# Layer 1's convolved inputs by seven block products instead of eight, and the norm ahead of the split

## The chip, the core and the metric

One core of a Trainium2 chip runs the whole program, two decoder layers for 528 positions. The metric is the device time of one execution in microseconds, the median of three runs. Five engines take part: PE (TensorE, matmuls), DVE (VectorE) and ACT (ScalarE) for element-wise work, POOL (GpSimd) and SP (SyncE), which issues nearly all DMAs. Each engine takes its instructions in the order in which they were placed on its queue, and waits at an instruction until what it needs is there.

## What is computed

16 meta positions are put ahead of 512 real ones (T = 528), the model width is 2048, all in float32. Layer 0 mixes with an S5 and an mLSTM branch; the change leaves it as it was up to its last output projection. Layer 1 is a Mamba-2 mixer:

```python
def ssd_layer(x, norm_g, w_in, conv_w, conv_b, dt_bias, a_log, d, gnorm, w_out):
    p = (rmsnorm(x, norm_g) @ w_in).astype(F32)
    z, xbc, dt = jnp.split(p, [SSD_INNER, SSD_INNER + SSD_CONV_DIM], axis=-1)
    xbc = jax.nn.silu(causal_dwconv(xbc, conv_w.astype(F32), conv_b.astype(F32)))
    xs, bm, cm = jnp.split(xbc, [SSD_INNER, SSD_INNER + SSD_GROUPS * SSD_STATE], axis=-1)
    ...
    def step(state, inp):
        xc, dtc, bc, cc = inp
        cum = jnp.cumsum(dtc * a, axis=1)
        seg = jnp.exp(jnp.where(causal, cum[:, :, None] - cum[:, None], -jnp.inf))
        cb = jnp.einsum('btgn,bsgn->btsg', cc, bc)
        w = cb[..., None] * seg * dtc[:, None]
        y = (jnp.einsum('btsgr,bsgrp->btgrp', w, xc)
             + jnp.exp(cum)[..., None] * jnp.einsum('btgn,bgrpn->btgrp', cc, state))
        ...
    y = y * silu(z); y = groupwise rmsnorm(y) * gnorm
    return x + y @ w_out
```

(The last two lines are shortened.) SSD_INNER is 4096; there are 8 groups, each with one tile of b, one of c, four of x and four of z, a tile being 128 channels by 528 positions. The states advance over chunks of 16, 128, 128, 128 and 128 positions. A final rmsnorm follows, and the meta positions are dropped.

## The kernel before

Channels lie on partitions, positions in the free dimension. A matmul operand of float32 is held as a high part `h` (rounded to fp32r) and a remainder `l`, and a product is three matmuls: h by h, h by l, l by h. So an activation `x` is a tile of 128 x 2 x 528, and a weight tile of 128 x 1024 (eight contraction tiles) is loaded as `wraw`, cast by ACT to `wh` and subtracted by DVE to `wl` (`wload`, L114), each with three buffers. `gemm` (L135) makes one output tile of 128 channels: 16 contraction tiles x two halves of 264 positions x three matmuls = 96 matmuls into two PSUM banks `g` of the pool `psg`, which has three; the banks are then emptied by the caller's `evac`.

The instructions' order on every queue is fixed when the program is built, by a planner that lists the program with a model of each engine's time; `tc.high_priority(offset=...)` pulls a piece forward in that list. What the code writes one after the other is therefore interleaved: in layer 1 PE's queue runs one group's SSD matmuls among the projection matmuls of z and of the next group.

*The seam.* `last0` (L1040) receives each of 16 output tiles of layer 0: it stores the stream, multiplies by the norm's weight `gp1` and splits the result at once into `x`, and adds the squares to `acc1`. The reciprocal root mean square `rstd` is known only after the last tile: a matmul with `ones` sums `acc1` over partitions (L1052), ACT takes the root and DVE the reciprocal. Since `x` is left unnormed, all projections run without waiting for `rstd`, and each evacuation multiplies by it: `xf<-g,rstd` (L1124), `zr<-g,rstd` (L1223). The first projection is dt's, 64 rows wide (L1091), then b, c and the four x tiles of group 0.

*A group.* `ssd_group_in` (L1129) calls `xbc` (L1121) for b, c and four x tiles: 96 matmuls, evacuation into `xf`, then the causal convolution and SiLU. c has only 516 positions, two halves of 258. `ssd_group` (L1147) transposes b and x on PE, builds the states, and then for each of four channel tiles i: a DMA brings the running sums of two heads, broadcast to all partitions, into `cr` (128 x 1024, two buffers, L1193 and 1195); DVE subtracts (`wexp<-cumc,cr`, L1199), ACT applies Relu and Exp, DVE multiplies by `cbm`; PE forms `p<-wexp,xdt` (L1206) and `p<-bc,state` (L1210); ACT makes `ecum`, the exponential of cr (L1212, 1213); DVE puts the two halves together into `yss` (L1215 to 1217). `ssd_out` (L1226) multiplies by the gate z, whose projection `ssd_z` (L1221) PE runs in between, and norms the group. Groups 0 to 6 run so in turn; group 7 runs beside the output projection.

Of the kernel before, what the change touches and what calls it, by code (L numbers as in the profile page):

```python
# [11 lines left out]
F32 = mybir.dt.float32  # L12
# [8 lines left out]
T = SEQ + N_META  # L21
# [3 lines left out]
REAL = ((N_META, SEQ),)  # L25
RMS_EPS, HEAD_EPS = 1e-6, 1e-5
# [15 lines left out]
def hybrid_trunk(ctx: ExitStack, tc: tile.TileContext, io, out):  # L42
# [931 lines left out]
    def out_steps(op, w, ys, k0, nk, cols, src, dst, between=lambda m: None, beside=1, ws={}, upto=KD):  # L974
# [3 lines left out]
        while todo:  # L978
            ms = [todo.pop(0) for _ in range(beside)]
            rs = []  # L980
            for _ in ms:
                res = op.tile([128, T], F32, tag="res", bufs=2, name="res")
                move(res[:, :n], src(_))
                rs.append(res)
# [13 lines left out]
            yield  # L998

# [16 lines left out]
    def fillers():  # L1016
# [5 lines left out]
        yield from out_steps(op, io["wo0"], ya, 0, 8, FULL, lambda m: io["hT"][:, m], lambda m, r_: move(o1D[:, m], r_), lambda m: len(yb) < 8 and load_b(m))  # L1022
# [3 lines left out]
        yield from out_steps(op, io["wo0"], yb, 8, 6, FULL, lambda m: o1D[:, m], lambda m, r_: move(o2D[:, m], r_), lambda m: [load_c(m) for _ in range(2) if len(yc) < 12], ws=ws)  # L1026
# [13 lines left out]
    def last0(m, res):  # L1040
        move(hD[:, m], res)
        x = xp.tile([128, 2, T], F32R, tag="x", name="x")
        split(x, res, gp1[:, m:m + 1])
# [5 lines left out]
    out_part(op, io["wo0"], yc, 20, 6, FULL, lambda m: o2D[:, m], last0)  # L1049
    ss = pair()  # L1050
    for hf, (c0, cn) in enumerate(FULL):
        mm(ss[:, hf, :cn], ones, acc1[:, c0:c0 + cn], True, True)  # L1052
    rstd_of(halves(rstd), ss[:, :, :HALF], 1.0 / D_MODEL, halves(acc1))
    p2.close()
    op_.close()
    xs = xs1

# [5 lines left out]
    op1 = o1.enter_context(tc.tile_pool(name="out1", bufs=1, reuse_waits="tile"))  # L1063
    p3 = ExitStack()
# [26 lines left out]
    gemm([io["wdt"]], xs, lambda hf, c0, cn, p: mul(xd[:, c0:c0 + cn], p, rstd[:SSD_H, c0:c0 + cn]), m=64, nk=16)  # L1091
# [25 lines left out]


    C_COLS = ((12, 258), (270, 258))

    def xbc(m, tag, bufs, cols=FULL):  # L1121
        xf = qp.tile([128, T + 3], F32, tag="xf", bufs=2, name="xf")
        G.memset(xf[:, 0:3 + cols[0][0]], 0.0)  # L1123
        gemm(w1(32 + m), xs, lambda hf, c0, cn, p: mul(xf[:, 3 + c0:3 + c0 + cn], p, rstd[:, c0:c0 + cn]), cols=cols)  # L1124
        o = qp.tile([128, T], F32, tag=tag, bufs=bufs, name=tag)
        conv_silu(xf, cw1[:, m], cb1[:, m:m + 1], o, True)
        return o

    def ssd_group_in(g):  # L1129
        b = xbc(32 + g, "bc", 4)  # L1130
# [305 lines left out]
```

## Time and profile before

| | us |
|---|---|
| median of three runs | 2892.97 (2890.85 to 2894.90) |
| the profiled execution | 2893.52 |
| its span | 2891.8 |
| PE busy in the span | 2853.4 (99%) |
| DVE busy | 2033.8 (70%) |
| ACT busy | 1240.7 (43%) |
| the seam: last matmul of layer 0 starts | 1451.47 |
| b and c of group 0 done | 1487.22 |
| one of five like groups of layer 1 | 131.5 |

The profile is that of one execution; times inside it are counted from its span's start. Records of one engine may overlap by some 0.1 us where they follow each other, and a matmul's record is longer than the distance to the next one, because matmuls are pipelined; the cost of a matmul is the distance. An F32 matmul leaves two records. The matmul clock that was granted stands beside each stretch as a share of 2.4 GHz.

### The profile page before, as it was taken

The page shows a single profiled execution, that of the slowest core. Times are in us where ns is not written, and L with a number is a line of the kernel's source. Part 1 is how long each engine was busy: PE and PEld are TensorE (multiplying, and loading weights), DVE is VectorE, ACT ScalarE, POOL GpSimd, SP SyncE. Part 2 cuts the span into 40 slices and gives each one's busy share as a digit, 9 for nine tenths or more (in the row PEclk, how much of TensorE's full clock was granted, in tenths as well). Part 3 has the DMA queues.
Part 4 walks back from the last instruction along what each step waited for, and adds up shares of the span by engine and source line. Part 5 has one row for each costly group of instructions (what it writes and reads, how often), then busy time and mean ns, then how long its engine had stood idle before and what let it go on. Part 6 is the DMA issues. An engine that isn't in the chain of part 4 may idle for free.

```text
span 2891.8 us, 50753 instructions
## 1 busy us (share of the span) xinstructions
PE 2853.4 (99%) x20483; PEld 2638.5 (91%) x20483; DVE 2033.8 (70%) x3343; ACT 1240.7 (43%) x2118; POOL 268.1 (9%) x550
## 2 busy tenths in 40 slices
PE   8999999999999999999999999999999999999998
PEld 8999999999999999999998989898998989788887
DVE  8998889889867766754466776767676767663333
ACT  7554445444336645533333443434352534332222
POOL 3122211220001111100000000000000000000000
PEclk9999999999999999999999999999999999999999
DMA  5333333333345666565543323333232323355433
GB/s 194 113 113 114 112 125 112 107 108 117 118 168 168 208 206 207 166 191 168 157 102 105 124 95 110 102 103 112 88 122 81 126 90 121 123 166 179 153 119 114
DMA packets 155599, 383.73 MB, mean 133 GB/s; under 512 B 18964, under 2 KB 37396, under 8 KB 155364
## 3 DMA queue, kind: packets, MB, share of 16 engines
q1 hardware_dynamic: 153188, 378.39, 40.9%
q8 instruction: 161, 2.64, 0.4%
q10 hardware_dynamic: 2176, 2.10, 0.2%
q14 instruction: 74, 0.61, 0.1%
HBM read 320.22 MB, written 60.20 MB: 132 GB/s over the span
## 4 chain that ended last, share of the span: by engine, by line
PE 86%; DMA 4%; DVE 4%; ACT 2%; issue 2%; POOL 1%; SPq 0%; DVEq 0%; ACTq 0%; POOLq 0%
PE g L74 76%; PE p L74 5%; PE s L74 2%; DMA wraw<-in_wo 1%; PE p L1206 1%; PE s L430 1%; DVE nm L47 1%; PE p L1171 1%; DVE nm L65 1%; ACT w L68 1%; DVE wl L47 1%; ACT wh L119 0%; DMA wraw<-in_w 0%; PE p L556 0%; DMA ae<-rowD 0%
## 5 line engine op out<-in xcount | busy, mean ns | idle before, releaser
L74 PE MATMUL g<-x,wh 128*128 128x264 f32 (+2 forms) x10176 | 2111.2, 303 | 14.7 <-ACT wh L286 5.8
L74 PEld LDWEIGHTS g<-x,wh 128*128 128x128 f32 x10176 | 1629.0, 188 | 96.5 <-issue 17.6
L74 PE MATMUL g<-x,wl 128*128 128x264 f32 (+2 forms) x5088 | 1534.4, 302 | 0.2 <-DVE wl L47 0.2
L74 PEld LDWEIGHTS g<-x,wl 128*128 128x128 f32 x5088 | 956.5, 188 | 33.8 <-issue 2.3
L119 ACT CAST wh<-wraw 128x1024 fp32r<-128x1024 f32 (+1 forms) x435 | 441.9, 1017 | 919.6 <-PE g L74 680.6
L47 DVE TENSOR_TENSOR wl<-wraw,wh 128x1024 fp32r<-128x1024 f32 (+2 forms) x444 | 529.9, 1194 | 266.0 <-ACT wh L119 261.9
L74 PE MATMUL g<-y,wh 128*128 128x264 f32 (+2 forms) x1312 | 296.3, 321 | 0.0
L74 PEld LDWEIGHTS g<-y,wh 128*128 128x128 f32 x1312 | 217.8, 188 | 20.2
L74 PE MATMUL g<-y,wl 128*128 128x264 f32 (+2 forms) x656 | 211.9, 323 | 0.0
L65 DVE SCALAR_TENSOR_TENSOR acc<-xf,cw,acc 128x528 f32<-128x528 f32 x216 | 172.8, 800 | 4.9 <-ACT acc L68 1.2
L47 DVE TENSOR_TENSOR res<-g,res 128x264 f32<-128x264 f32 (+2 forms) x129 | 62.8, 489 | 117.6 <-PE g L74 112.6
L74 PEld LDWEIGHTS g<-y,wl 128*128 128x128 f32 x656 | 123.4, 188 | 9.1
L47 DVE TENSOR_TENSOR xf<-g,rstd 128x264 f32<-128x264 f32 (+1 forms) x142 | 59.6, 424 | 84.8 <-PE g L74 84.4
L68 ACT ACTIVATE wexp<-wexp 128x1024 f32<-128x1024 f32 x64 | 67.7, 1058 | 53.3 <-DVE wexp L47 51.4
L418 ACT CAST us<-hl 32x264 fp32r<-32x264 f32 x192 | 78.8, 411 | 6.3 <-PE p L74 3.5
L1123 POOL MEMSET xf<- 128x3 f32 (+1 forms) x48 | 5.0, 105 | 714.9 <-DVE acc L65 508.7
L68 ACT ACTIVATE acc<-xf,cb,cw 128x528 f32<-128x528 f32 x72 | 59.4, 825 | 26.8 <-DVE xf L47 26.8
L47 POOL TENSOR_TENSOR dec<-decx,dec 128x512 fp32r<-128x512 f32 (+1 forms) x32 | 46.9, 1464 | 240.9 <-ACT dec L1178 240.9
L47 DVE TENSOR_TENSOR y<-wraw,y 128x512 fp32r<-128x512 f32 (+1 forms) x28 | 19.5, 699 | 65.6 <-ACT y L126 65.5
L68 ACT ACTIVATE tab<-tab,ec 128x32 f32<-128x32 f32 (+3 forms) x128 | 41.5, 331 | 48.8 <-POOL tab L47 48.8
L68 ACT ACTIVATE x<-acc 128x528 f32<-128x528 f32 x32 | 20.6, 645 | 80.2 <-DVE acc L65 80.2
L47 DVE TENSOR_TENSOR acc<-g,rstd 128x264 f32<-128x264 f32 (+1 forms) x64 | 28.0, 437 | 35.9 <-PE g L74 35.3
(1000 smaller groups left out, 3092.1 us busy)
## 6 DMA issues: line engine op xcount, KB each, us to landing
wraw<-in_w SPq DMA_DIRECT2D x285, 512.0 KB, 3.5
wraw<-in_wo SPq DMA_DIRECT2D x80, 512.0 KB, 4.0
wraw<-in_wo SPq DMA_DIRECT2D x64, 384.0 KB, 3.6
cr<-cumD SPq DMA_DIRECT2D x32, 512.0 KB, 4.7
zD<-s SPq DMA_DIRECT2D x32, 264.0 KB, 2.0
y1D<-yss SPq DMA_DIRECT2D x32, 256.0 KB, 2.1
wraw<-y1D SPq DMA_DIRECT2D x32, 256.0 KB, 2.9
xcD<-xc SPq DMA_DIRECT2D x24, 264.0 KB, 2.1
```

Of the source, the lines that this page charges most:

```text
L47: (eng or V).tensor_tensor(out=out, in0=a, in1=b, op=op)
L65: V.scalar_tensor_tensor(out=out, in0=a, scalar=s, in1=b, op0=op0, op1=op1)
L68: S.activation(out=out, in_=a, func=func, **kw)
L74: PE.matmul(o, lhsT=w, rhs=x, start=start, stop=stop)
L119: S.copy(h[:, :n], raw[:, :n])
L418: S.copy(us[32 * n:32 * n + 32, q], hl[rows, a].bitcast(F32))
L430: PE.matmul(yps[32 * q:32 * q + 32, :HALF], lhsT=c[:, n, 32 * q:32 * q + 32], rhs=x[:, n], start=n == 0, stop=n == 1, tile_position=(0, 32 ...
L1123: G.memset(xf[:, 0:3 + cols[0][0]], 0.0)
L1171: PE.transpose(out=o[:, 128 * i:128 * i + 128], in_=x[i][:, s0:s0 + sn_], identity=ident)
L1206: PE.matmul(yp[64 * r_:64 * r_ + 64, 0, 128 * ch:128 * ch + 128], lhsT=xdt[:, ch, 64 * (2 * i + r_):64 * (2 * i + r_) + 64], rhs=w[:, r_, ...
```

## The change

Three things are changed, all in layer 1 and at its beginning.

1. The norm is applied to the stream. `last0` keeps `x` as plain F32 (no split). After the last tile, `rstd` is made in two halves, dt's projection runs with F32 operands from the unnormed x (32 matmuls into a `p` pair, in the place of 96 into `g`), and then each of the 16 tiles is multiplied by `rstd` (`normed`) and split (`finish`). The evacuations multiply by nothing; z's `silu2` reads PSUM directly.
2. b and c, and the x tiles two by two, are made in pairs by `gemm_pair`. Two output tiles by two halves of positions by two blocks of contraction tiles (three tiles each, NP = 3) is a 2 x 2 by 2 x 2 block product; it is formed by seven block products in Winograd's arrangement. It needs four combinations of x (made once, tiles `t`, by twelve differences `tr` and their splits) and four of the weights (`wsum`, five DVE operations of 384 columns a pair, then splits of 768). The other 10 contraction tiles are added in as before. The banks are asked for one at a time: p1, p2, p3, p6, p7, p5, p4, q4. 23 pairs are made so; b and c of group 0 are made in the old way, without pairs.
3. Buffers shrink to make room: `cr` has one buffer and its exponential is written into it (`ecum` is gone), `bc` has three for four, `yss` four for five, `decx` shares with `ysqa`, `res` of the last projection shares with `t`.

Cut to its core:

```diff
     def last0(m, res):
         move(hD[:, m], res)
-        x = xp.tile([128, 2, T], F32R, tag="x", name="x")
-        split(x, res, gp1[:, m:m + 1])
+        x = xp.tile([128, T], F32, tag="x", name="x")
+        act(x, res, AF.Identity, scale=gp1[:, m:m + 1])
...
-    rstd_of(halves(rstd), ss[:, :, :HALF], 1.0 / D_MODEL, halves(acc1))
+    with tc.high_priority(offset=1500):
+        for hf, (c0, cn) in enumerate(FULL):
+            c_ = slice(c0, c0 + cn)
+            mm(ss[:, hf, :cn], ones, acc1[:, c_], True, True)
+            rstd_of(rstd[:, c_], ss[:, hf, :cn], 1.0 / D_MODEL, acc1[:, c_])
...
+    dps = pair()
+    for k, x in enumerate(xs1):
+        for hf, (c0, cn) in enumerate(FULL):
+            mm(dps[:SSD_H, hf, :cn], wdt[:, k], x[:, c0:c0 + cn], k == 0, k == KD - 1)
...
+        for k in range(NP):
+            a, b = normed(k, "xf", 2), normed(k + NP, "bc", 3)
+            finish(k, a)
+            finish(k + NP, b)
+            tr = qp.tile([128, 4, HALF], F32, tag=("xdt", "state")[k % 2], name="tr")
+            sub(tr[:, 0], a[:, HALF:], a[:, :HALF])
...
+            split(t, tr)
+            tf.append(t)
+        for k in range(2 * NP, KD):
+            finish(k, normed(k, *(("xf", 2), ("bc", 3))[k % 2]))
...
+        p1 = bank()
+        prod(p1, g1, 0, xq(0, lo), True, True)
+        with tc.high_priority(offset=1500):
+            S.copy(f2[:, hi], p1[:, :HALF])
+        p2, p3 = bank(), bank()
...
+        g3 = wpart(s2s4, 2 * NS)
+        p6 = bank()
+        prod(p6, g3, 0, tq(1), True, True)
+        evac(f2[:, hi], f2[:, hi], p6)
+        prod(p3, g3, NS, xq(1, hi), False, True)
+        evac(f1[:, hi], f2[:, hi], p3)
...
+        p7, p5 = bank(), bank()
+        prod(p7, g4, 0, tq(2), True, True)
+        evac(f2[:, lo], f2[:, hi], p7)
+        prod(p5, g4, NS, tq(0), True, True)
+        evac(f1[:, hi], f1[:, hi], p5)
...
     def ssd_group_in(g):
-        b = xbc(32 + g, "bc", 4)
-        c = xbc(40 + g, "bc", 4, C_COLS)
+        b, c = xbc((32 + g, 40 + g), "bc", 3, g == 0)
+        x = xbc((4 * g, 4 * g + 1), "x2", 6) + xbc((4 * g + 2, 4 * g + 3), "x2", 6)
...
-            cr = qp.tile([128, 2, 4, 128], F32, tag="cr", bufs=2, name="cr")
+            cr = qp.tile([128, 2, 4, 128], F32, tag="cr", bufs=1, name="cr")
...
-            ec_ = qp.tile([128, SEQ], F32, tag="ecum", bufs=1, name="ecum")
-            act(ec_[0:64], cr[0:64, 0].rearrange("p c t -> p (c t)"), AF.Exp)
+            ec_ = cr[:, 0].rearrange("p c t -> p (c t)")
+            act(ec_[0:64], ec_[0:64], AF.Exp)
...
-        gemm(w1(m), xs, lambda hf, c0, cn, p: mul(z, p, rstd[:, c0:c0 + cn]), cols=REAL)
-        silu2(z, z, th)
+        gemm(w1(m), xs, lambda hf, c0, cn, p: silu2(z, p, th), cols=REAL)
```

How the instructions stand on the queues shows at two places. On PE at the seam, before, the sum of squares (`p<-acc,ones_r`) stands deep among dt's narrow matmuls (`g<-x,wh 64x264`):

```order
L74 MATMUL g<-x,wh 64x264 x2
L74 MATMUL g<-x,wl 64x264
L74 MATMUL g<-x,wh 64x264
L74 MATMUL p<-acc_16474,ones_r 128x264 x2
L74 MATMUL g<-x,wh 64x264
```

After, on the same engine and place, from the last matmuls of layer 0 (`g<-y_16471`) to the first of b:

```order
L76 MATMUL g<-y_16471,wh 128x264 x2
L76 MATMUL g<-y_16471,wl 128x264
L76 MATMUL p<-acc_16474,ones_r 128x264
L76 MATMUL p<-x,wdt 64x264 x11
L76 MATMUL p<-acc_16474,ones_r 128x264
L76 MATMUL p<-x,wdt 64x264 x21
L76 MATMUL g<-x,wh 128x264 x4
```

The first sum of squares now stands directly behind layer 0's last matmul, with nothing between it and the addition into acc that it reads.

On DVE in the middle of a steady group's core, before (`yss<-p,ecum` begins the use of one product of the four, `wexp<-cumc,cr` the making of a decay matrix from a loaded cr):

```order
L47 TENSOR_TENSOR yss<-p,ecum 128x512
L47 TENSOR_TENSOR zr<-g,rstd 128x512
L47 TENSOR_TENSOR yss<-yss,p 128x512
L47 TENSOR_TENSOR wexp<-cumc,cr 128x1024
L65 SCALAR_TENSOR_TENSOR yss<-x_22418,dsk,yss 128x512
L65 SCALAR_TENSOR_TENSOR zr<-zth,zr 128x512
L47 TENSOR_TENSOR yss<-p,ecum 128x512
L47 TENSOR_TENSOR wl<-wraw,wh 128x1024
L47 TENSOR_TENSOR yss<-yss,zr 128x512
L47 TENSOR_TENSOR wexp<-cumc,cr 128x1024
```

After, between the second and the third product of a group (`xf<-xf,g` is an addition that empties a bank of a pair, `wl<-wsum,wh` the split of a weight sum):

```order
L49 TENSOR_TENSOR yss<-p,cr 128x512
L49 TENSOR_TENSOR yss<-yss,p 128x512
L49 TENSOR_TENSOR xf<-xf,g 128x264
L67 SCALAR_TENSOR_TENSOR yss<-x_22567,dsk,yss 128x512
L49 TENSOR_TENSOR yss<-yss,zr 128x512
L49 TENSOR_TENSOR wexp<-cumc,cr 128x1024
L49 TENSOR_TENSOR wl<-wsum,wh 128x768
L49 TENSOR_TENSOR ysqa<-ysqa,zth 128x512
L49 TENSOR_TENSOR wl<-wraw,wh 128x640
L49 TENSOR_TENSOR wexp<-wexp,cbm 128x1024
```

Before, a decay matrix is begun while products that use the other cr buffer are still to come; after, each `wexp<-cumc,cr` stands behind the `yss<-p,cr` that frees the one buffer, with the load of cr between the two.

## Rows read from the trace of the kernel before

**Rows 1.** The page: busy us of each engine, share of the span, instructions.

```profile
PE 2853.4 (99%) x20483; PEld 2638.5 (91%) x20483; DVE 2033.8 (70%) x3343; ACT 1240.7 (43%) x2118; POOL 268.1 (9%) x550
```

**Rows 2.** By stretch: us; busy PE, PEld, DVE, ACT, POOL; clock; DMA share; GB/s.

```profile
1475.72:1487.22 11.50, 11.50 (x98) 11.50 (x97) 10.84 (x18) 3.48 (x4) 0.24 (x1) 1.00 0.42 138
1487.22:1534.06 46.84, 46.84 (x386) 46.63 (x384) 31.70 (x46) 16.30 (x26) 1.17 (x10) 1.00 0.51 113
1678.80:1810.30 131.50, 131.50 (x911) 118.67 (x910) 93.65 (x113) 53.82 (x67) 7.75 (x11) 1.00 0.32 105
```

**Rows 3.** PE's two longest waits, 1440 to 2890: us, times, longest.

```profile
PE p L1206 <- DVE wexp L47: 2.2, 1, 2.2
PE g L74 <- DVE zr L47: 1.0, 1, 1.0
```

**Rows 4.** Timeline at the seam: start us, length us, engine, line, operation, [idle before].

```profile
1451.60 0.40 PE L74 MATMUL g<-x,wh 128*64 128x264 f32 x2
...
1453.94 0.76 DVE L65 SCALAR_TENSOR_TENSOR x<-res,gp,x 128x528 fp32r<-128x528 f32 x1
...
1454.62 0.70 DVE L47 TENSOR_TENSOR acc<-acc,sg 128x528 f32<-128x528 f32 x1
...
1457.84 1.05 PE L74 MATMUL p<-acc,ones_r 128*128 128x264 f32 x4
1458.54 0.48 PE L74 MATMUL g<-x,wh 128*64 128x264 f32 x1
1458.85 0.28 PE L74 MATMUL g<-x,wl 128*64 128x264 f32 x1
...
1459.66 3.45 DVE L172 RECIPROCAL rstd<-acc 128x528 f32<-128x528 f32 x1 [4.34 <-ACT acc L68]
...
1464.06 0.41 PE L74 MATMUL g<-x,wh 128*128 128x264 f32 x2
```

**Rows 5.** Timeline of ACT and DVE in a steady group's core, same columns.

```profile
2117.64 2.16 ACT L68 ACTIVATE wexp<-wexp 128x1024 f32<-128x1024 f32 x2 [0.85 <-DVE wexp L47]
2119.70 1.26 ACT L68 ACTIVATE ecum<-cr 64x512 f32<-64x512 f32 x2
...
2122.85 1.22 DVE L47 TENSOR_TENSOR wexp<-wexp,cbm 128x1024 f32<-128x1024 f32 x1
2123.99 0.69 DVE L47 TENSOR_TENSOR zr<-g,rstd 128x512 f32<-128x512 f32 x1
2124.59 0.69 DVE L47 TENSOR_TENSOR ysqa<-ysqa,zth 128x512 f32<-128x512 f32 x1
```

**Rows 6.** Groups by shape, 1440 to 2890: operation, count | busy us, mean ns | idle before.

```profile
L47 DVE TENSOR_TENSOR wl<-wraw,wh 128x1024 fp32r<-128x1024 f32 x225 | 281.9, 1253 | 165.5 <-ACT wh L119 165.5
...
L47 DVE TENSOR_TENSOR xf<-g,rstd 128x264 f32<-128x264 f32 x80 | 34.3, 430 | 81.6 <-PE g L74 81.5
...
L47 DVE TENSOR_TENSOR bt<-s,bt 128x384 fp32r<-128x384 f32 x8 | 4.4, 552 | 1.0 <-ACT bt L126 1.0
...
L581 DVE RECIPROCAL x<-x 64x528 f32<-64x528 f32 x1 | 3.4, 3444 | 0.0
```

**Rows 7.** Tile cr: its DMA's time from issue to landing, and DVE's idle for it.

```profile
  DMA cr<-cumD: 21.5, 9
...
DMA to landing us min/median/max: 4.0/4.7/10.7
```

**Rows 8.** Two idle times of PE, and the clock after each, by stretch.

```profile
90.16 0.73 PE L74 MATMUL g<-x,wh 128*128 128x264 f32 x2 [2.75 <-DVE u L47]
...
91.00:92.00 1.00, 1.00 (x6) 1.00 (x6) 1.00 (x7) 1.00 (x2) 0.00 (x0) 0.50 0.47 184
...
93.00:94.00 1.00, 1.00 (x8) 1.00 (x8) 1.00 (x5) 1.00 (x5) 0.00 (x0) 0.66 0.00 0
...
1602.89 1.09 PE L1206 MATMUL p<-wexp,xdt 128*64 128x128 f32 x16 [2.19 <-DVE wexp L47]
...
1602.00:1604.00 2.00, 1.11 (x17) 0.97 (x17) 2.00 (x4) 0.56 (x1) 0.00 (x0) 1.00 0.00 0
```

## What the change does to the time: the prediction

> **What bounds the kernel now.** I read the page first: the engines' row [rows 1]. PE is busy for 99% of the span, so a us of PE work saved is a us of time saved, as long as nothing new makes PE wait. Second, the table by stretch [rows 2]: one steady group of layer 1 takes 131.5 us with PE busy for all of it, DVE for 93.7 and ACT for 53.8; the row of 46.84 us holds four x tiles, 386 matmuls, 0.1213 us from one to the next (0.122 below). Third, what PE waited for from 1440 us on [rows 3]: 2.2 and 1.0 us in 1450, and no other wait worth a row. So the kernel before gives PE its operands in time everywhere, with 38 us of DVE's slack per group; the question is what that cover is worth after. The profiled execution took 2893.52 us (span 2891.8), 0.55 above the median of the three runs, 2892.97; the sum is made against it. About 0.2%, 5.8 us, is what a measurement here can tell from no change.
>
> **The change part by part.**
>
> *Fewer matmuls.* By the order of the two kernels, PE has 207 fewer 264-column matmuls: 207 x 0.122 = 25.3 us. The 768 matmuls of c had 258 columns and have 264: six columns at 0.122/264 each, +2.1; 98 of them took 11.50 us before [rows 2], 0.117 each with gaps, which would give more, but neither is over 4. I take +1.5. Sum: **-23.8**. This is certain to within 3 us.
>
> *The seam between the layers.* Before, x was split as it was made and left unnormed, so the b projection only waited for the 96 narrow matmuls of wdt (1451.60 to 1464.06, 12.5 us), and the norm ran beneath them; b and c were done at 1487.22, where x begins [rows 2, 4]. After, PE's next instruction behind the last out0 matmul is the ones matmul of the first half, on acc. Acc was ready at 1454.62 + 0.70; without the l part of the last x (0.76 before it) at about 1454.7: PE stands for 3.1 us. Then 11 wdt matmuls in F32, the second ones matmul, 21 more. An F32 matmul of 264 columns costs 0.444: from 1457.84 to 1458.85 lie two of them and one plain one [rows 4]; 32 are 14.2 us. They end at 1469.9, but x isn't there: the second half's ones end at 1460.5, its sqrt and reciprocal (half of 3.45) at 1463.05. Only then does DVE start on what b needs, in this order: 16 products of 128x528 and 16 l parts (0.62 each from one to the next, its 0.70 less 0.08 of overlap, as rows of 512 lie 0.60 apart [rows 5]: 19.8), 12 differences of 264 (0.34: 4.1), three l parts of 1056 (1.17, from 1.14 for 1024: 3.5), the reciprocal of softplus that stands among them (3.4 [rows 6]), a weight split (1.1) and six small ones (some 4): 36 us. The last x tile is split at 1498.9; b and the first half of c follow tile by tile, then 48 matmuls of c's second half (5.9) and the rest of the last tile: 1505.5 against 1487.22, **+18.3**. The 3.1 us and the F32 price lie inside it. From below: had the six small ones and the reciprocal fallen in gaps, 11; from above, 22. The first pair starts into DVE's backlog of the same stretch: its p3 is added into xf at 1522.8 by the queue, and p5 wants the bank at 1518.3: **+4.5** (0 to 6).
>
> *One cr buffer for two.* The steady group's core is four products yp0 to yp3; yp(i+1) needs the decay matrix wexp made from cr. With two buffers cr(i+1) is loaded while i is used. With one, and the exponential written into it, the load can start only when DVE has multiplied yp(i) by cr. The chain, with durations from [rows 5 to 7]: PE's last product to the multiply 0.3, multiply 0.69, issue 0.1, DMA 4.65 (median 4.7), subtract 1.22, relu 1.0, then on ACT's queue ahead of the second exponential the two exponentials of cr (1.26) and a weight cast of 640 (0.7), the exponential 1.06, DVE's product 1.22: 12.2, or **12.0 us** with the overlap of records that follow each other. In its shortest form, DMA 4.0 and no cast and no exponentials between, 9.4; with a DMA of 6, 13.4. What PE has to do meanwhile is counted from the order: between yp0 and yp1 11.5 us (0.5 to 0.9 short with what DVE has queued: 0.75), between yp1 and yp2 52 matmuls, 6.3 us less the state products counted in the chain, 6.2 (5.6 to 5.8 short: 5.6), between yp2 and yp3 10.4 to 11.4 (1.2 short). **7.5 us a group, six groups: +45.3**, and 1.3 in the first set, whose matmuls between are longer. Shortest 3.2 x 6 = 19; longest 12 x 6 = 72. The last group has 15 us between its products: nothing. While DVE stands at `wexp<-cumc,cr` its queue stands too: before, the same instruction waited for its DMA nine times, 21.5 us in all [rows 7], at no cost to PE. Behind it now are weight splits and the additions of the pair, which give PE's banks back.
>
> *The clock.* An idle of 2.75 us that ended at 90.16 was followed by a granted clock of 0.50, 1.2 GHz, into the stretch at 93, which has 0.66: some 3.3 us at half speed, about 1.6 lost; an idle of 2.19 us at 1600.7 left it at 1.00 [rows 8]. The idle of 5.6 us in each of six groups is over both: 6 x 1.6 = **+9.6** (0 to 16). Beside it the Trainium skill (TensorE: Matmul & The Clock Gate, "Why this matters for your kernels") says the same of gaps between bursts of matmuls: the clock goes back to half. By it the term stays; without it the sum is 9.6 less.
>
> *One bank at a time.* A pair asks for p1, p2, p3, p6, p7, p5, p4, q4 in a ring of three banks of psg. p5 takes p3's, and p3's sum must go through DVE after p6's; PE has only p7 in between, 9 matmuls, 1.1 us. Two additions of 264 take 0.43 + 0.34 if DVE is free, and it isn't: per group it loses 2.7 us of z products and gains 15 weight sums of 384 (0.55), 24 additions for 12 evictions (0.43), and 4.5 us of splits (a pair's four of 1024 become three, one of 640 and two of 768; 1.25 for 1024, the others by their width): 93.7 + 15 = 109 of 128 us. Walking the queue through three pairs gave waits of 1.4, 0.55 + 1.6 and 2.3: 5.9 a group. After a wait for cr DVE has caught up, so I take half: 3 a group, seven groups, **+21**; bounds 0 and 41.
>
> *At nothing:* z goes through tanh straight from the bank (ACT and DVE then hold it about 1.5 us, three banks cover it; if not, 0.5 a tile, 16); bc, yss and decx have fewer buffers, last needed a full group earlier; the out stage takes its res from t's three buffers.
>
> Sum: 2893.5 - 23.8 + 18.3 + 4.5 + 45.3 + 1.3 + 9.6 + 21 = **2969.7**.
>
> **The rivals.**
> *The chain is hidden (faster).* If the pair's work did cover cr between yp1 and yp2, and the additions met a free DVE, only the seam is left: 2893.5 - 23.8 + 15 = 2885, and 2888 with my seam. It decides where the chain is under 6.2 us. For it: ACT is only 41% busy in a group. Against: the load alone never landed in under 4.0 us, and with one subtract, two ACT passes and one product it is 9.4. It is the weakest of the cases.
> *The chain at its shortest,* 3.2 us a group, clock kept, seam 15, no bank waits: 2893.5 - 23.8 + 15 + 3 + 19 = 2907. For it: DVE that waits for cr has nothing else to do when it lands.
> *Everything full:* the walk's 41 for the banks, and the long chain: 2969.7 + 20 + 27 = 3017. For it: DVE at 85% with PE's banks behind it.
> *The clock falls in each pair.* If the bank waits, short but many, too brought the clock to 1.2 GHz, 23 pairs x 1.6 = 37 more: 3007. Against: the row of 2.19 us at 1.00 [rows 8]. The Trainium skill (the same page, "A second HAM failure mode: psum-queue depth-cycling") describes short idles between groups of matmuls through cycled banks doing this; no row here shows it.
>
> **How the numbers follow.** My case 0.58; chain at its shortest 0.14; full 0.08; clock in each pair 0.06; hidden, 0.10 (most of it under 2887), and between it and the shortest 0.04. So faster 0.09, same 0.05, slower 0.86. The range leaves out the hidden case and the upper end of the last two: 2908 to 3010.
>
> **What would show it.** In the profile after: PE busy near 96%, with waits on `wexp` (line of yp's first product) of some 5 to 6 us once a group and a granted clock of 0.5 just behind; a stretch from 1451.6 to the end of c of 54 us for 35.6; DVE's idle ahead of `wexp<-cumc,cr` at 6 to 7 us a group, ended by the DMA of cr; short waits of `g` on DVE's `xf`. A group's period would be 131.5 - 3.1 + 7.5 + 1.6 + 3 = 140.5. I am wrong if the period is under 129 (chain and banks hidden), if b and c end before 1495 (the seam isn't DVE's), or if 1.2 GHz never shows in the steady groups.

## The result, and the profile after

The changed kernel takes 2990.28 us (median of four runs, 2986.32 to 2993.64) against 2893.93 of the kernel before on the same chip: a ratio of 1.0334, with a 95% interval of 1.0316 to 1.0352. It is slower by 96 us, where the forecast was slower by 76; the time lies within the range. The profiled execution took 2986.32 us, its span is 2984.5, 92.7 above the span of before.

The engines' row of the page after, to be read beside [rows 1]; columns are busy us, share of the span and instructions:

```profile
PE 2871.0 (96%) x20244; PEld 2639.7 (88%) x20244; DVE 2124.7 (71%) x3590; ACT 1287.7 (43%) x2212; POOL 267.0 (9%) x550
```

PE has 239 instructions fewer and is busy for 17.6 us *more*, and it idles besides: both have to be explained. Two stretches of after by window (us; busy PE, PEld, DVE, ACT, POOL; clock; DMA share; GB/s), the seam and one steady group, to be read beside the third of [rows 2]:

```profile
1447.34:1504.48 57.14, 47.49 (x260) 38.22 (x260) 50.56 (x78) 25.63 (x37) 0.20 (x2) 0.85 0.10 31
1753.48:1895.79 142.31, 132.64 (x882) 118.40 (x882) 103.04 (x143) 58.25 (x76) 7.56 (x11) 0.97 0.30 97
```

From the last matmul of layer 0 to the last of c are 57.4 us (1447.09 to 1504.48), where 35.6 were; a group takes 142.3 for 131.5. What PE waited for from 1440 us on (us, times, longest), where before had 3.7 us in all:

```profile
PE g L76 <- DVE xf L49: 23.4, 27, 3.6
PE p L1352 <- DVE wexp L49: 21.8, 6, 4.5
PE g L76 <- ACT xf L1216: 20.8, 12, 5.7
PE g L76 <- DVE x L49: 6.2, 5, 2.5
PE p L76 <- DVE acc L49: 3.1, 1, 3.1
PE g L76 <- DVE zr L67: 2.1, 1, 2.1
```

With four small ones these are 80.5 us. `xf` stands for the banks of the pairs (DVE's additions and ACT's copy of p1, L1216, empty them), `wexp` for the decay matrices, and the next two rows for the seam.

**Where the 92.7 us come from.** Fewer matmuls -23.8, as worked out before. Waits of PE +76.8 (80.5 less 3.7). The clock: from 1440 us on there are 14 stretches, some 75 us together, at 1.2 GHz, with PE at work in 64 of them; half of that, 32, is lost, and before had no such stretch there. Around each wait PE loses some 0.15 us more than the idle that the record gives (7.0 us over the 47 waits between 1505 and 2600 us), some 9 in all: a matmul's record is 0.28 us long, and the idle is counted from its end, while in a steady row the next matmul starts 0.12 us behind its start. The F32 matmuls of dt +2.4. Layer 0, whose order on PE is the same, came out 4.4 us shorter in this execution (1447.09 for 1451.47); over the profiles of all the kernels here its last matmul starts anywhere from 1444.26 to 1452.90, so 4 us are within the scatter. These sum to 92.0.

**The seam.** PE's wait for acc, the first products of the norm, the softplus reciprocal that stands among them, the last split of x and the last matmul of c (start us, length us, engine, line, operation, idle before):

```profile
1450.44 0.68 PE L76 MATMUL p<-acc,ones_r 128*128 128x264 f32 x2 [3.06 <-DVE acc L49]
...
1460.88 0.71 DVE L49 TENSOR_TENSOR xf<-x,rstd 128x528 f32<-128x528 f32 x1
...
1479.15 3.44 DVE L583 RECIPROCAL x<-x 64x528 f32<-64x528 f32 x1
...
1495.83 0.70 DVE L49 TENSOR_TENSOR x<-bc,x 128x528 fp32r<-128x528 f32 x1
...
1504.48 0.28 PE L76 MATMUL g<-x,wl 128*128 128x264 f32 x1
```

From 1460.88 to 1495.83 DVE works through multiplications, splits, differences and the reciprocal, and b and c follow at its pace. The five rows are the forecast's list, in its order.

**The chain of cr.** One of the long waits. These are the steps from the multiplication that frees the one buffer to the product that needs the next decay matrix; the rows at 2329.78 and 2330.26 are no steps of it, but an addition of a pair and the wait of PE for it:

```profile
2328.26 0.69 DVE L49 TENSOR_TENSOR yss<-p,cr 128x512 f32<-128x512 f32 x1 [3.81 <-PE p L76]
...
2329.01 0.38 SPq L73 DMA_DIRECT2D cr<-cumD  x1
...
2329.78 0.43 DVE L49 TENSOR_TENSOR xf<-xf,g 128x264 f32<-128x264 f32 x1
...
2330.26 0.51 PE L76 MATMUL g<-x,wh 128*128 128x264 f32 x2 [0.59 <-DVE xf L49]
...
2333.02 1.23 DVE L49 TENSOR_TENSOR wexp<-cumc,cr 128x1024 f32<-128x1024 f32 x1 [1.42 <-DMA cr<-cumD]
...
2334.28 1.06 ACT L70 ACTIVATE wexp<-wexp 128x1024 f32<-128x1024 f32 x1 [1.74 <-DVE wexp L49]
...
2335.25 1.25 ACT L70 ACTIVATE cr<-cr 64x512 f32<-64x512 f32 x2
...
2336.52 0.72 ACT L1184 CAST wh<-wraw 128x640 fp32r<-128x640 f32 x1
2337.15 1.05 ACT L70 ACTIVATE wexp<-wexp 128x1024 f32<-128x1024 f32 x1
...
2338.24 1.22 DVE L49 TENSOR_TENSOR wexp<-wexp,cbm 128x1024 f32<-128x1024 f32 x1
...
2339.61 1.97 PE L1352 MATMUL p<-wexp,xdt 128*64 128x128 f32 x16 [4.29 <-DVE wexp L49]
```

11.35 us from the first row to the last, the forecast's chain step for step (12.0 with the 0.3 that lie ahead of the first row); the load takes 4.0 for the 4.65 assumed. Behind the last product of the tile before (its next matmul starts at 2327.97) PE has 7.35 us until it stands, 6.6 of work and 0.75 around the wait at 2330.26, for the 6.2 counted. So PE stands for 4.3 here. Of the six waits five are like this one (4.2 to 4.5 us, once in each of five groups); the sixth is 0.2.

**A second wait on the same chain.** The queues of SP, DVE and ACT a few us earlier, in the same group:

```profile
2313.10 0.38 SPq L73 DMA_DIRECT2D cr<-cumD  x1
...
2316.96 1.22 DVE L49 TENSOR_TENSOR wexp<-cumc,cr 128x1024 f32<-128x1024 f32 x1
...
2318.21 1.06 ACT L70 ACTIVATE wexp<-wexp 128x1024 f32<-128x1024 f32 x1 [2.17 <-DVE wexp L49]
...
2319.18 1.25 ACT L70 ACTIVATE cr<-cr 64x512 f32<-64x512 f32 x2
...
2320.46 0.83 ACT L1171 CAST wh<-wsum 128x768 fp32r<-128x768 f32 x1
2321.19 1.05 ACT L70 ACTIVATE wexp<-wexp 128x1024 f32<-128x1024 f32 x1
...
2322.15 0.36 ACT L1216 COPY xf<-g 128x264 f32<-128x264 f32 x1
...
2322.56 0.52 PE L76 MATMUL g<-x,wh 128*128 128x264 f32 x2 [1.94 <-ACT xf L1216]
```

The copy that empties p1's bank stands last of these five rows of ACT, and PE waits 1.94 us for that bank. The record names ACT and `xf`; what made the copy late stands above it in its queue: ACT had waited 2.17 us for DVE's difference. That one started without an idle of DVE, behind other work of DVE, some 0.2 us after the load of cr had landed (issued at 2313.10, 3.7 us), so the load and DVE's queue came to it nearly together. Six of the twelve waits are of this kind, 1.94 to 2.00 us, 11.7 together; the longest, 5.75 us at 1546.05, is the same order of instructions behind the first load of cr, for which DVE stood 7.57 us. This is the part that the forecast had not seen.

### The profile page after: what moved, and what is told of

The parts are those of the page before. It is cut to its first block, busy times and chain, and to the rows that moved or that the text cites. A ratio compares the mean times of both kernels' runs of the same rounds, so it can differ in the third digit from the quotient of the medians.

```text
span 2984.5 us, 50779 instructions
## 1 busy us (share of the span) xinstructions
PE 2871.0 (96%) x20244; PEld 2639.7 (88%) x20244; DVE 2124.7 (71%) x3590; ACT 1287.7 (43%) x2212; POOL 267.0 (9%) x550
## 3 DMA queue, kind: packets, MB, share of 16 engines
q1 hardware_dynamic: 153188, 378.39, 39.6%
## 4 chain that ended last, share of the span: by engine, by line
PE 75%; DVE 10%; DMA 7%; ACT 4%; issue 3%; POOL 1%; SPq 0%; DVEq 0%; ACTq 0%; POOLq 0%
PE g L76 65%; PE p L76 5%; DMA wraw<-in_wo 2%; DVE wl L49 2%; DMA cr<-cumD 2%; PE s L76 2%; PE p L1352 1%; DVE wexp L49 1%; DVE yss L49 1%; PE s L432 1%; ACT wexp L70 1%; DVE nm L49 1%; DVE x L49 1%; DVE xf L49 1%; ACT wh L121 1%
## 5 line engine op out<-in xcount | busy, mean ns | idle before, releaser
L76 PE MATMUL g<-x,wh 128*128 128x264 f32 (+1 forms) x9422 | 1984.9, 306 | 41.8 <-ACT xf L1216 11.7
L76 PEld LDWEIGHTS g<-x,wh 128*128 128x128 f32 x9422 | 1523.2, 189 | 128.3 <-issue 14.9
L76 PE MATMUL g<-x,wl 128*128 128x264 f32 (+1 forms) x4711 | 1431.6, 305 | 0.3 <-DVE wl L49 0.3
L76 PEld LDWEIGHTS g<-x,wl 128*128 128x128 f32 x4711 | 891.7, 190 | 36.4 <-issue 4.8
L49 DVE TENSOR_TENSOR wl<-wraw,wh 128x1024 fp32r<-128x1024 f32 (+3 forms) x443 | 513.2, 1159 | 251.3 <-ACT wh L121 209.1
L76 PE MATMUL g<-t,wh 128*128 128x264 f32 x552 | 114.5, 305 | 25.0 <-DVE xf L49 12.3
L76 PEld LDWEIGHTS g<-t,wh 128*128 128x128 f32 x552 | 91.2, 200 | 32.1 <-ACT xf L1216 10.4
L49 DVE TENSOR_TENSOR xf<-xf,g 128x264 f32<-128x264 f32 x184 | 75.2, 423 | 19.4 <-PE g L76 14.1
L76 PE MATMUL g<-t,wl 128*128 128x264 f32 x276 | 81.6, 296 | 0.0
L49 DVE TENSOR_TENSOR res<-g,res 128x264 f32<-128x264 f32 x96 | 40.8, 428 | 45.2 <-PE g L76 40.5
```

Of the source, the lines that this page charges most:

```text
L49: (eng or V).tensor_tensor(out=out, in0=a, in1=b, op=op)
L76: PE.matmul(o, lhsT=w, rhs=x, start=start, stop=stop)
```

## The experiments

All times are medians, beside the kernel before on the same chip; what a run gives back is counted as the difference of two such distances, from the 96 us of the changed kernel. The diffs are cut to their core. Each edit is built anew, and the planner then lays a new order on every queue: a run shows what a buffer and the order laid for it do together.

**1. Two cr buffers in the changed kernel** (one `wexp` buffer makes the room; the exponential is still written into cr).

```diff
-            cr = qp.tile([128, 2, 4, 128], F32, tag="cr", bufs=1, name="cr")
+            cr = qp.tile([128, 2, 4, 128], F32, tag="cr", bufs=2, name="cr")
...
-            w = qp.tile([128, 2, 4, 128], F32, tag="wexp", bufs=2, name="wexp")
+            w = qp.tile([128, 2, 4, 128], F32, tag="wexp", bufs=1, name="wexp")
```

> The changed kernel with two buffers of cr again, paid for by one buffer of wexp for two; all else as it is. Theory A (the load of cr inside the chain between two products is what stops PE, directly and by DVE's additions and ACT's copies that stand behind it on their queues): the waits on wexp (21.8 us in the changed kernel) and on ACT's copies (20.8) go to under 10 together, the stretches at 1.2 GHz in the steady groups go with them, and the time is 2925 to 2950. With one wexp the chain from product to product is subtract, Relu, Exp, multiply, about 4.6 us, under the 6.2 us of PE work. Theory B (the pair's three banks and DVE's load stop PE, and cr only decides at which instruction it shows): the waits move to xf and g, and the time is 2970 to 2995.

2923.38 us, before 2891.24: ratio 1.0106 (1.0090 to 1.0121). PE's waits:

```profile
PE g L76 <- ACT xf L1216: 22.5, 7, 4.3
...
PE g L76 <- DVE xf L49: 1.4, 2, 0.8
...
PE p L1352 <- DVE wexp L49: 0.9, 4, 0.3
```

The waits for `wexp` go from 21.8 to 0.9, as the chain demands, and those on DVE's `xf` go with them, from 23.4 to 1.4, although DVE is busy for as long (103.5 us in a group of 133.3). So most of what the forecast charged to DVE's load was the order on DVE's queue. What DVE stood for in five steady groups points to where: at the multiplication by cr, for PE's product, 39.6 us (19 times) after and 11.0 us (5 times) here; for the load of cr only 9.1 and 4.0. With one buffer the next load waits for this multiplication, and additions stand behind it on DVE's queue, as the one at 2329.78 above. Some 64 us come back. A copy of p1 for which PE waits 3 us a group is left, with 1.2 GHz behind it, so theory A missed that part; the time lies just under its range.

**2. One cr buffer in the kernel before**, with the exponential in place.

```diff
-            cr = qp.tile([128, 2, 4, 128], F32, tag="cr", bufs=2, name="cr")
+            cr = qp.tile([128, 2, 4, 128], F32, tag="cr", bufs=1, name="cr")
...
-            ec_ = qp.tile([128, SEQ], F32, tag="ecum", bufs=1, name="ecum")
-            act(ec_[0:64], cr[0:64, 0].rearrange("p c t -> p (c t)"), AF.Exp)
+            ec_ = cr[:, 0].rearrange("p c t -> p (c t)")
+            act(ec_[0:64], ec_[0:64], AF.Exp)
```

> The kernel before with the one part alone: cr in one buffer and its exponential written into it. Theory A: the chain of multiply, load (4.0 to 4.7 us), subtract, two ACT passes and product, 10 to 12 us, stands between products that have 0, 10.4 and 8.7 us of PE work between them in the old order, so PE waits 4 to 10 us a group with a stretch at 1.2 GHz behind it: 2920 to 2965. Theory B: without pairs the order finds enough work for PE to lay between: 2890 to 2900.

2897.24, before 2891.24: 1.0019 (1.0009 to 1.0028), a cost of 6 us. The tile's row for cr (DVE's idle ahead of it, us and times), and PE's waits:

```profile
  DMA cr<-cumD: 40.5, 30
```

```profile
PE g L74 <- DVE xf L47: 5.1, 7, 1.0
PE g L74 <- DVE zr L47: 4.2, 1, 4.2
PE p L1206 <- DVE wexp L47: 2.4, 2, 1.5
```

Theory A missed, and theory B holds. DVE now waits 30 times for the load, 40.5 us, more than the 32.1 us (14 times) of after, and PE hardly feels it. With one buffer the planner lays another order here: in a steady group the products lie 16.8 to 25 us apart, where in the kernel before the second and third lie 11.8 apart and the third and fourth 10.8. In the changed kernel the second and third lie 13.6 us apart, from start to start, with 9.3 us of work. From product to product the chain lasts 13.6 (2.2 us from the product to the multiplication, and the 11.35 above). So the single buffer costs PE a wait only where the order leaves less work between two products than that.

**3. The norm on the stream alone**: no pairs, two cr buffers, the exponential still in place.

```diff
-        if plain:
+        if True:
...
-            cr = qp.tile([128, 2, 4, 128], F32, tag="cr", bufs=1, name="cr")
+            cr = qp.tile([128, 2, 4, 128], F32, tag="cr", bufs=2, name="cr")
```

> The norm applied to the stream and then split, dt's projection in F32, no pairs (no t, no weight sums, each tile by 96 matmuls), cr in two buffers. Theory A (the seam is bound by DVE's queue between the second reciprocal and the last split): without the 12 differences and 3 splits of t (7.6 us) it is 13 to 15 us longer than before, and six columns more in c's matmuls cost 1.5: 2904 to 2912. Theory B (the seam is long because of the t work and the waits between tiles, the norm itself lies under dt's and b's matmuls): 2893 to 2899.

2926.82, before 2891.24: 1.0122 (1.0106 to 1.0137); both theories missed. One wait stands out:

```profile
PE g L76 <- DVE zr L67: 15.3, 8, 6.7
```

**3b. The same, with the exponential in a tile of its own.**

```diff
-            ec_ = cr[:, 0].rearrange("p c t -> p (c t)")
-            act(ec_[0:64], ec_[0:64], AF.Exp)
+            ec_ = qp.tile([128, SEQ], F32, tag="ecum", bufs=1, name="ecum")
+            act(ec_[0:64], cr[0:64, 0].rearrange("p c t -> p (c t)"), AF.Exp)
```

> The run with the norm alone, with the exponential of cr in a tile of its own. That run came out 35 us over the kernel before, of which the seam shows only two waits of 3.1 and 3.5 us; its other waits ended at DVE's reading of z's bank, which stood behind a subtraction that waited for cr. Theory A (the exponential in place holds both cr buffers until the product is used): 2901 to 2912. Theory B (z read twice from its bank is what holds PE): 2918 to 2930, the same as there.

2906.74, before 2893.79: 1.0047 (1.0032 to 1.0062). The wait on `zr` is gone. So reading z straight from its bank costs PE no wait here, as forecast; what made it late in run 3 was a `wexp` difference ahead of it on DVE's queue that waited for cr (for 2.29 us at 1611.30, 3.55 at 1882.90, 3.63 at 2149.74). The in-place exponential holds a buffer until DVE has multiplied by it; that costs some 23 us even with two buffers. The norm alone costs 13 us.

**4. The pairs alone**: buffers as in the changed kernel, the norm as before. x is split unnormed, the twelve differences are made from h + l, and `rstd` is multiplied onto each pair's tile and into z.

```diff
         else:
             gemm_pair(ms, xfs)
+            for xf in xfs:
+                mul(xf[:, 3:], xf[:, 3:], rstd)
...
-        gemm(w1(m), xs, lambda hf, c0, cn, p: silu2(z, p, th), cols=REAL)
+        gemm(w1(m), xs, lambda hf, c0, cn, p: mul(z, p, rstd[:, c0:c0 + cn]), cols=REAL)
+        silu2(z, z, th)
```

> The pairs and the small buffers without the norm on the stream: x is split unnormed as before, t is made from it while b and c run, and rstd is multiplied in later (once a tile of a pair on DVE, and for z as before: some 6 us of DVE work a group more). Theory A: the seam's 21 us go and DVE's extra work gives some of it back: 2965 to 2978. Theory B (DVE's load is what stops PE in the groups): the extra 6 us a group on DVE take back more than the seam gives: 2985 to 3010.

2975.55, before 2891.24: 1.0285 (1.0268 to 1.0303), in theory A's range. Without the new norm most of the loss is still there. Its largest row of waits is

```profile
PE g L76 <- DVE xf L49: 37.9, 35, 3.3
```

**5. Run 4 with the exponential in its own tile, one `wexp` buffer and three `xf` buffers** (cr keeps one).

```diff
-        xf = qp.tile([128, T + 3], F32, tag="xf", bufs=2, name="xf")
+        xf = qp.tile([128, T + 3], F32, tag="xf", bufs=3, name="xf")
...
-            w = qp.tile([128, 2, 4, 128], F32, tag="wexp", bufs=2, name="wexp")
+            w = qp.tile([128, 2, 4, 128], F32, tag="wexp", bufs=1, name="wexp")
...
-            ec_ = cr[:, 0].rearrange("p c t -> p (c t)")
+            ec_ = qp.tile([128, SEQ], F32, tag="ecum", bufs=1, name="ecum")
```

> The kernel with pairs but without the norm on the stream, and with two bounds lifted: the exponential of cr goes into a tile of its own again, so cr is free before the product is used, and xf has three buffers for two (paid for by one wexp for two). The run with two buffers of cr lost 22.5 us on ACT's copies of p1 into xf, which waited for the last convolution that read that xf buffer. Theory A (in-place cr and two xf buffers are what holds PE's banks): waits of PE behind layer 0 under 20 us, 2875 to 2897. Theory B (DVE's load, 6 us a group more here, is the bound): 2905 to 2945.

2911.05, before 2893.79: 1.0060 (1.0045 to 1.0075), between the two forecasts. A steady group is 132.85 us with DVE busy for 107, where run 7 with the same buffers, below, has 128.0 and 103. Bank waits stay, so here DVE's load is not ruled out as their cause:

```profile
PE g L76 <- DVE xf L49: 17.3, 9, 3.9
PE g L76 <- ACT xf L1192: 9.4, 6, 2.5
```

**6. The changed kernel with only the exponential's tile** (and one `wexp` buffer for room).

```diff
-            w = qp.tile([128, 2, 4, 128], F32, tag="wexp", bufs=2, name="wexp")
+            w = qp.tile([128, 2, 4, 128], F32, tag="wexp", bufs=1, name="wexp")
...
-            ec_ = cr[:, 0].rearrange("p c t -> p (c t)")
-            act(ec_[0:64], ec_[0:64], AF.Exp)
+            ec_ = qp.tile([128, SEQ], F32, tag="ecum", bufs=1, name="ecum")
+            act(ec_[0:64], cr[0:64, 0].rearrange("p c t -> p (c t)"), AF.Exp)
```

> The changed kernel with one bound lifted: the exponential of cr in a tile of its own (and one wexp, to make room); cr keeps one buffer and xf two. Theory A (cr held until the product is used is the large part, the two xf buffers the small one): the waits on wexp go, ACT's copies of p1 still wait for xf, 2.5 to 3.5 us a group with 1.2 GHz behind them, as in the run with two cr: 2915 to 2930. Theory B (the xf buffers are the large part): 2945 to 2980.

2909.82, before 2891.68: 1.0065 (1.0050 to 1.0080). Still with one cr buffer, 78 of the 96 us come back, more than the second buffer of run 1 gave; the time lies below theory A's range. The load now starts when ACT has read cr, not when DVE has multiplied by it. DVE's standing at that multiplication is 7.5 us (5 times) in five steady groups for 39.6, and for the load of cr it stands as long as after (8.6 for 9.1). In a steady group PE waits only 1.0 to 1.4 us for the copy of p1.

```profile
PE g L76 <- ACT xf L1216: 13.9, 8, 4.4
...
PE g L76 <- DVE xf L49: 1.9, 6, 0.3
PE p L1352 <- DVE wexp L49: 1.2, 1, 1.2
```

**7. Run 6 and a third `xf` buffer.**

```diff
-        xf = qp.tile([128, T + 3], F32, tag="xf", bufs=2, name="xf")
+        xf = qp.tile([128, T + 3], F32, tag="xf", bufs=3, name="xf")
```

> The changed kernel, norm on the stream and all, with the same two bounds lifted (exponential of cr in its own tile, three xf, one wexp). Theory A: the 22.5 us of ACT's copies in the run with two cr buffers (2923) and the 1.2 GHz behind each go: 2885 to 2905; what is left over the 23.8 us saved is the seam. Theory B (ACT's and DVE's load): it stays at 2915 to 2930.

2892.01 (ten runs), before 2893.79: 0.9994 (0.9985 to 1.0004), no change that can be told, and in theory A's range. Its steady group and its seam by window, and PE's two largest waits:

```profile
1748.00:1876.00 128.00, 128.00 (x885) 115.43 (x885) 103.07 (x143) 58.98 (x76) 7.89 (x11) 1.00 0.33 108
1448.36:1504.69 56.33, 46.24 (x262) 37.51 (x261) 50.02 (x77) 25.89 (x37) 0.30 (x3) 0.88 0.10 32
```

```profile
PE g L76 <- DVE x L49: 5.0, 2, 2.7
PE p L76 <- DVE acc L49: 3.1, 1, 3.1
```

The group is 128.00 us with PE busy for all of it: the 3.5 us that the pairs save per group are real, and DVE's 103 us of work do not make PE wait in it. The p1 copy of run 1 had waited for an `xf` buffer of the pair before, still held by its convolution (ACT stood 2.27 us for DVE's `acc` ahead of the copy at 1787.95); so had run 6's copy at 1660.09 (1.97 us), while the shorter waits of its steady groups end at a copy that stands behind a weight sum's cast. With the third buffer and the order laid for it both are gone. What eats the gain is the seam: c ends 56.3 us behind layer 0 for 35.6, 20.7 later, against 3.5 x 6 = 21 saved in the groups behind it.

**8. Run 4 with two contraction tiles to a block (NP = 2) and all buffers**: cr 2, `xf` 3, the exponential in its own tile.

```diff
-NP = 3
+NP = 2
...
-            cr = qp.tile([128, 2, 4, 128], F32, tag="cr", bufs=1, name="cr")
+            cr = qp.tile([128, 2, 4, 128], F32, tag="cr", bufs=2, name="cr")
```

> Pairs of two contraction tiles for three (4 of 16 tiles by seven products, six matmuls saved a pair for nine: 138 x 0.122 = 16.8 us), norm at the end as before, and with the room this leaves two cr, two wexp, the exponential in its own tile and three xf. Theory A: no bound is left but the pair's additions: 2875 to 2892. Theory B (the pair's additions and DVE's load stop PE in any case, two to three us a pair): 2900 to 2950.

2915.99, before 2893.79: 1.0082 (1.0067 to 1.0097), in theory B's range. No `wexp` waits to speak of (1.1), but the copy of p1 has 16.7 us in seven waits and the additions 8.9. With smaller blocks and the norm as before the banks come back too late although the buffers are there; which of the two does it, this run doesn't separate.

**9. Run 7 with another seam**: all 16 tiles multiplied and split first, the differences made afterwards from h + l, the softplus of dt put behind b and c, and b and c made side by side.

```diff
+        for k in range(KD):
             finish(k, normed(k, *(("xf", 3), ("bc", 3))[k % 2]))
+    for k in range(NP):
+        a, b = (qp.tile([128, T], F32, tag=tag, bufs=3, name=tag) for tag in ("xf", "bc"))
+        for o, x in ((a, xs[k]), (b, xs[k + NP])):
+            add(o, x[:, 0].bitcast(F32), x[:, 1].bitcast(F32))
...
         b, c = xbc((32 + g, 40 + g), "bc", 3, g == 0)
+        if g == 0:
+            dt_rows()
```

> The run with both bounds lifted (2892) and a shorter queue on DVE at the seam: all 16 tiles of x are multiplied and split first, t is made after them (from h plus l again, six additions more), softplus of dt comes behind b and c, and b and c are made together, tile by tile, into two banks of g and a p pair, so that no 48 matmuls are left when the last tile comes. Theory A (DVE's queue between the second reciprocal and the last split sets the seam): it shortens from some 57 us to 42 to 46, and the time is 2872 to 2882. Theory B (the work moved is late for the first pair of x tiles, and the wait only moves there): 2886 to 2896.

2895.37, before 2891.68: 1.0009 (0.9999 to 1.0018): the time is theory B's. b and c end earlier, as theory A wanted:

```profile
1448.42:1492.43 44.01, 40.95 (x262) 33.34 (x261) 38.33 (x57) 20.14 (x29) 0.10 (x1) 0.96 0.12 40
```

but the first product of group 0 comes 132.8 us behind layer 0, where run 7 has 131.0 and before 116.3. Ahead of it, at the first pair of x tiles, PE stands 3.4 us for the l part of t, 0.7 for its h part and 3.3 for the copy of p1, with 10.2 us at 1.2 GHz from 1509 on. The work taken from ahead of b is what that pair needs.

**10. Run 9 with part of the norm and all of the differences on POOL.**

```diff
-            mul(x, xs1[k], rstd)
+            tt(x, xs1[k], rstd, ALU.mult, G if k % 3 == 2 else None)
...
-            add(o, x[:, 0].bitcast(F32), x[:, 1].bitcast(F32))
+            tt(o, x[:, 0].bitcast(F32), x[:, 1].bitcast(F32), ALU.add, G)
```

> The run with the shorter seam queue (2895, where the wait moved to t and the first pair), with part of the same work given to POOL: 5 of the 16 multiplications by rstd, and for t the six additions of h and l and the twelve differences. On DVE 11 products, 16 l parts and 3 splits of t stay, some 20 us for 31. Theory A (the sum of DVE's work between the second reciprocal and the first use of t is the seam, wherever it stands): b and c keep PE's pace of 1.46 us a tile, t is there in time, 2872 to 2884. Theory B (POOL is too slow, some 1.5 us a product and 0.75 a difference, or slows DVE beside it, and the tiles and t come as late as before): 2888 to 2898.

2900.17, before 2892.32: 1.0024 (1.0013 to 1.0035), above both ranges. That is some 4 us slower than run 9, each counted from its own kernel before, and the first product comes after 139.6 us. Two products of one shape on DVE, the second beside the one on POOL:

```profile
1458.05 0.71 DVE L49 TENSOR_TENSOR xf<-x,rstd 128x528 f32<-128x528 f32 x1
1458.16 1.76 POOL L49 TENSOR_TENSOR xf<-x,rstd 128x528 f32<-128x528 f32 x1 [218.95 <-DVE rstd L174]
1458.68 1.81 DVE L49 TENSOR_TENSOR bc<-x,rstd 128x528 f32<-128x528 f32 x1
```

DVE takes 1.81 us for 0.71 while POOL's runs. POOL is no place for this work. The Trainium skill (SBUF — State Buffer, "SBUF: two separate sides") says that DVE, in an operation with two SBUF inputs, and GpSimd take a port pair in turns, each for a whole instruction. The trace agrees: 1.10 us are added, and DVE's product ends 0.57 us behind POOL's.

**11. Run 7 with the softplus held back until b's first value is there** (its bias takes zero times that value), b and c side by side, the differences early as in run 7.

```diff
+    def dt_rows(b):
+        nonlocal cum, dec
+        stt(dtb2, b[:SSD_H, 0:1], 0.0, dtb, ALU.mult, ALU.add)
+        mul(halves(xd), dps[:SSD_H, :, :HALF], halves(rstd[:SSD_H]))
+        ts(xd, xd, dtb2, ALU.add)
...
         b, c = xbc((32 + g, 40 + g), "bc", 3, g == 0)
+        if g == 0:
+            dt_rows(b)
```

> The run with both bounds lifted (2892), t made early as there, and dt's softplus held back until the first value of b is there (a bias that adds zero times b), so that its reciprocal of 3.4 us and some 3 us of small operations leave DVE's queue ahead of the last split; b and c are made together into two banks of g and a p pair, so that no 48 matmuls are left at the end. Theory A (DVE's queue ahead of the last split is the seam, and only work that can go elsewhere without hurting shortens it): the last split comes some 6 us earlier, b and c end with it instead of 6 us after, 2878 to 2888. Theory B (the softplus then delays the first pair or the first cr, and the seam's gain is given back there): 2890 to 2900.

2892.32 (eleven runs), before 2892.07: 1.0002 (0.9993 to 1.0011), in theory B's range. b and c end after 46.0 us, and the first product comes after 142.8: the late rows of dt are now what it waits for (`state`, `dec` and `dtb` stand among PE's waits, 2.6, 2.1 and 1.2 us). Three arrangements of the seam, runs 7, 9 and 11, so end within 3.4 us of one another (ratios 0.9994, 1.0009 and 1.0002). None beats the kernel before.

## Why the prediction was right, point by point

*Fewer matmuls, -23.8.* Right: 128.0 for 131.5 us a group where nothing waits (run 7); in the changed kernel it is hidden under the waits.

*The seam.* The mechanism and the order were right: 21.8 us for the forecast's 18.3, within 3.5. DVE is busy for 50.6 of its 57.1 us. What was not priced is the clock inside it: 1.2 GHz for 3.4 us behind the wait for acc, and again where PE works in short pieces (us; busy PE to POOL; clock; DMA share; GB/s):

```profile
1481.00:1496.00 15.00, 11.38 (x50) 10.77 (x51) 14.94 (x23) 4.56 (x7) 0.14 (x2) 0.54 0.10 35
```

At 0.54 some of b and c runs at half speed. PE loses some 7 us so at the seam, half of the 14.3 us that it works at 1.2 GHz. Of the second stretch most is hidden, since DVE gives the pace. The first is not: the 11 F32 matmuls from 1451.05 to 1457.78 take 6.73 us, where the forecast's price makes 4.9, and `rstd`'s second half and DVE's first product come later by as much.

*The first pair, +4.5.* The wait for p5's bank did not come; at 1519.78 PE stands 1.13 us for a weight's cast.

*The chain of cr.* Right in place, length and releaser between the second and the third product; 21.8 us in all, for 46.6. There 5.6 us were forecast, and 4.3 came: the load was shorter by 0.65, and PE's cover longer by the 0.75 around a bank's wait and by 0.4 of work. The 0.75 and 1.2 us at the other two pairs of products, and the 1.3 of the first set, did not come at all. DVE's idle for the load, forecast at 6 to 7 us a group, is 9.1 us in five groups: DVE stands at the multiplication instead.

*One bank at a time, +21.* The waits are there, 44.2 us on `xf` (20.8 and 23.4), and the reason given was wrong: not DVE's load by itself, which was 103 us a group for the 109 forecast. Runs 1 and 6 take the additions' waits away (1.4 and 1.9 left) by freeing cr sooner, and run 7 the copy's by a third `xf` buffer, while DVE keeps its 103 us. So the copy and the additions stood behind steps of the chain of cr: the multiplication that waits for PE's product, and ACT's passes over the decay matrix. Not all of them: the waits of 2.0 us at 2099.80 and 2386.93 end at additions behind a run of other DVE work. The chain's price, taken with what stands behind it and the order that the planner lays for it, is 78 us by run 6; the forecast's terms that hang on it, 45.3 + 1.3 + 9.6 + 21, make 77.

*How near the sum came.* That it was short by only 20 us is in part luck, for errors of both signs cancel: the waits for `wexp` were 25 us too high, the waits for banks 23 too low, the clock 22 too low, and the 9 us around waits were not in it. The parts are tied to one another, as run 6 shows, but the forecast did not say so.

*The clock, +9.6.* Too small: 32, of which some 7 at the seam. Only six falls had been counted. Behind the copy's wait of 1.94 to 2.00 us the clock fell in three groups (1894, 2034 and 2178) and not in three others (1752, 2322 and 2464). Two of these waits, and then the stretches behind them (same columns):

```profile
1752.23 0.52 PE L76 MATMUL g<-x,wh 128*128 128x264 f32 x2 [1.94 <-ACT xf L1216]
...
1894.51 0.55 PE L76 MATMUL g<-x,wh 128*128 128x264 f32 x2 [1.94 <-ACT xf L1216]
```

```profile
1752.30:1755.00 2.70, 2.70 (x22) 2.70 (x23) 1.81 (x3) 0.00 (x0) 0.00 (x0) 1.00 0.11 21
1895.00:1898.00 3.00, 3.00 (x16) 3.00 (x15) 1.39 (x3) 0.00 (x0) 0.00 (x0) 0.50 0.32 96
```

16 matmul records in 3.00 us at 0.50, 22 in 2.70 at full speed. Behind the `wexp` waits of 4.2 to 4.5 us it fell each time, as forecast (0.50 from 2339.60 to 2343.00). That [rows 8] had 2.19 us without a fall was no bound. The rival of a fall in every pair went too far: 14 stretches, not 29. The Trainium skill (TensorE: Matmul & The Clock Gate, "A second HAM failure mode: psum-queue depth-cycling") tells of short idles through cycled banks that lower the clock. The row at 1895 agrees, since a bank's copy ended that idle; the row at 1752 doesn't. In run 6, whose steady groups have the copy's wait at 1.0 to 1.4 us, the clock never falls in them.

*At nothing.* z straight from its bank: right (run 3b; run 7 has 2.9 us of such waits, in the first group). `xf`, which keeps two buffers while the pairs use them two at a time, should have stood in this list and did not; it is worth some 20 us, from run 6 to run 7.

*A group's period.* Forecast 140.5, measured 142.5 as the mean of five: -3.5 of matmuls, 9.5 of waits (10.5 forecast), 4 of the clock (1.6) and 1.1 of edges around waits (none).

**What stays open.** Why equal waits left different clocks. What makes the banks late in runs 5 and 8. How much of what each buffer gave back is the buffer, and how much the order that the planner laid for it: no run keeps the order and changes a buffer alone.

## What to carry to other kernels

Before a buffer is made to serve two ends, ask until when its new second use holds it, and what has to be loaded into it then: one tile for the exponential gave back 78 of 96 us, and with it went waits that the record put down to other tiles. A wait names the engine that came last; the instructions ahead of that one on its queue say why it came last. And when work is moved to a place where one engine sets the pace, count all that this engine must do before the next stage's first product: three orders of the seam's work ended within 3.4 us, as each moved the wait to another tile.

## What the runs showed of the hardware that was not expected

The clock was at 1.2 GHz behind a wait of 1.94 us and at 2.4 GHz behind an equal one. A DVE product of 128x528 took 1.81 us beside POOL's and 0.71 as that began.
